# Interleaved split queries and keys, three loads for a head's operands, and a list scheduler with new instruction lengths

## The chip, the cores and the metric

The kernel runs on one core of one Trainium2 chip. The metric is device time in microseconds (us) of one execution. Before the change the median of three runs is 2257.74 us (2257.31 to 2260.61).

## The reference, cut to what matters

One encoder layer over 1024 tokens of width 1024, in float32: a half-step SwiGLU FFN, then attention beside an RWKV-7 scan on one joint input projection, then a second half-step FFN, each with RMSNorm before and after.

```python
x = x + 0.5 * post1(FFN1(pre1(x)))
z = pre2(x) @ w_in                       # 3456 columns: q|k|v and the RWKV inputs
x = x + post2(concat(attn, rwkv) @ w_out)
x = x + 0.5 * post3(FFN2(pre3(x)))
```

The attention has 8 heads of 64, rotary positions, and three dilated bands centred on the query. For the two narrow bands a query tile of 128 needs the scores

```python
s = jnp.einsum('bhrnqd,bhrnkd->bhrnqk', qb, kb)   # q . k over 64 dimensions
```

The RWKV-7 group runs a delta-rule scan over the sequence in both directions, for 8 heads.

## The kernel before, in words

**Precision by splitting.** TensorE multiplies in fp32r, a shortened float32. An f32 operand is split into a high part h (a copy cast to fp32r, on ScalarE) and a low part l (the rest, on VectorE), and a product is summed from h h, h l and l h. For the narrow-band scores the depth is only 64, so two parts are stacked to use all 128 rows of the array: `sq` holds q's high part on rows 0 to 63 and its low part on rows 64 to 127; `kh` holds k's high part twice and `kl` its low part twice. sq by kh plus sq by kl is (qh + ql)(kh + kl). `near` does these two matmuls for each piece of the scores (lines 1150 and 1151).

**Where these operands come from.** `project_tokens` (line 930) computes K, Q and V for the 8 token tiles and two groups of 256 columns each (16 units for each of the three, in the order K, Q, V). For a unit of K or Q it multiplies on TensorE, applies rotary positions on VectorE, turns the result on TensorE (`zt`) and makes three tiles of it: `zts` (f32), `zth` (high) and `ztl` (low), each of two buffers. Each goes to its own DRAM tensor with one GpSimd-issued store (lines 959 and 960): `q_d` and `kt_d` are lists of three, [4, 128, S], for f32, high and low. V's units take one store each (`d_va`).

`stacked` (line 1121) loads a head's operands when its turn comes: six loads on SyncE's queue, each of 64 rows of 4 KB. The wide band (`far`) works from the f32 copies, `qp` and `kp`, which are loaded for two heads at once with 128 rows.

**The stages.** FFN1; the RWKV projections (`zr` in the profile); the token projection (`zq`); attention and the scan side by side; the output projection; FFN2. In the scan, `prep` builds matrices of a block of tokens (`lp`, `lm`, `bp`), writes a part of them to DRAM (`d_x`), and `solve` (line 1316) loads them as `X` and inverts them in 31 pairs of short dependent steps (`ttmp`, `Ti`), on GpSimd for blocks 1 to 5 and on VectorE for blocks 0, 6 and 7. The result goes through DRAM (`d_t`, `d_tt`) into `merge` (`d`, `tt`, matmuls `pa`, `pb`), and `chain` carries the state (`xu`, `y`, `st`).

**Who sets the order.** The program is first written on a tape (`_Tape`, line 100); `order` (line 460) then plans the order of all instructions of the five queues (tensor, vector, scalar, gpsimd, sync) with a list scheduler, and `play` (line 486) issues them in that order. That is why every row of the profile has line 491. The planner works with a length of each instruction (`cost`, line 257): `took` is how long it holds its engine, `late` what passes after that until another engine can use the result, `moved` how long a transfer holds the DMA engines. `lag` (line 317) gives the delay from one instruction to one that depends on it; before the change that is zero on the same engine, transfers excepted. Among the ready instructions of a queue the one with the highest rank is taken (the longest way to the end, refined over five sweeps). The sweep has its own model of TensorE's clock, in 3413 ns steps. `LEADS` (line 37) is a table of (first, last, amount) by which the ranks of ranges of instructions are shifted before the last sweep.

Of the kernel before, what the change touches and what calls it, by code (L numbers as in the profile page):

```python
# [32 lines left out]
def _ap(src, off, pat):  # L33
# [3 lines left out]
LEADS = (  # L37
# [10 lines left out]
)  # L48
# [51 lines left out]
class _Tape:  # L100
# [156 lines left out]
    def cost(self, op):  # L257
# [8 lines left out]
        if op.method == "dma_start":  # L266
            runs = [math.prod(q[1] for q in a.ap) // (a.ap[-1][1] if a.ap[-1][0] == 1 else 1) for a in (x, *op.ins)]
            size = math.prod(q[1] for q in x.ap) * 4
            half = any(a.tensor.name in self.home and a.ap[0][1] <= 64 for a in (x, *op.ins))
            op.took, op.late = (560 if op.eng == "gpsimd" else 360) + 200 * half, 1500 + (600 if half else 0)  # L270
            op.moved = (14 * max(runs) + 0.0384 * size) / 16
        elif op.eng == "tensor":
# [13 lines left out]
            op.grid, op.cell = (up(k), up(m)), (at(w), at(x) if m <= 64 else 0)  # L286
            op.late = 170
        elif op.eng == "vector":
            rate = 1.04
            if op.method in ("tensor_copy", "tensor_scalar", "memset") and all(  # L290
                    self.home.get(a.tensor.name, (None,))[0].space != PSUM for a in op.ins if a.tensor.name in self.home):
                rate = 0.52
            if op.method in ("tensor_tensor_reduce", "tensor_reduce"):
                n = max(n, max(math.prod(q[1] for q in a.ap[1:]) for a in op.ins))
            if op.method == "tensor_tensor_scan":
                rate = 2.1
            op.took, op.late = 150 + rate * n + (83 if "accum_out" in op.kwargs else 0), 35
            op.port = sum(self.home.get(a.tensor.name, (None,))[0].space is None for a in op.ins
                          if a.tensor.name in self.home and math.prod(q[1] for q in a.ap[1:]) > 1) > 1
            if op.method == "reciprocal":  # L300
                op.took = 150 + 5 * n
        elif op.eng == "scalar":
            func = op.args[2] if op.method == "activation" else None
            aps = sum(isinstance(op.kwargs.get(k), bass.AP) for k in ("scale", "bias"))
            op.took = 170 + 0.87 * n + 95 * aps + (188 if "accum_out" in op.kwargs else 0)
            op.load, op.late = LOADS.get(func, 0), 40
        else:
            op.took, op.late, op.port = (200 + 2.1 * n if op.method != "memset" else 130 + 0.8 * n), 40, op.method != "memset"

    def pace(self, last, op, idle):  # L310

        took = op.took
        if op.grid != (128, 128) and (last is None or last.grid != op.grid or last.cell != op.cell):
            took /= 2
        return took + 95 if last and last.grid != op.grid and idle < 100 else took

    def lag(self, p, s):

        if p.eng is None or p.eng == s.eng and p.method != "dma_start":
            return 0.0  # L320
        return p.late + p.moved + (200 if s.eng == "gpsimd" else 0)

# [22 lines left out]
    def sweep(self, back=False):  # L345
# [29 lines left out]
        follow, last, port = None, None, 0.0  # L375
        while True:
# [26 lines left out]
            while op is None and heap[e]:  # L403
# [5 lines left out]
                if tag:  # L409
# [5 lines left out]
                    if at > t + 1e-6:  # L415
                        push(later[e], (at, -op.rank, op.n, op))
                        op = None
                        continue
                    slots[tag].remove(at)
            if op is None:  # L420
# [14 lines left out]
            if op.port:  # L435
                t = max(t, port)
                port = t + took
            op.start = t
            own = free[e] = t + took
            end = own  # L440
            if op.moved and not back:
                wire = max(wire, own) + op.moved
                end = wire - op.moved
            op.end = end
            out.append(op)
# [190 lines left out]
class _Kernel:  # L636
# [293 lines left out]
    def project_tokens(self, p, psum, x):  # L930

        nc, V, A, G, T = self.nc, self.nc.vector, self.nc.scalar, self.nc.gpsimd, self.nc.tensor
        for b, g in [(b, g) for b in (1, 0, 2) for g in range(2)]:
            hl = self.columns(p, b * 512 + g * 256, 256)
            for t in range(NT):
# [16 lines left out]
                for i in range(2):  # L952
                    T.transpose(q[:, i, :], of[:, i * 128:(i + 1) * 128], self.ident)
                y, h, l = (p.tile([128, 2, 128], dt, name="z" + n, tag="z" + n, bufs=2)
                           for n, dt in (("ts", F32), ("th", F32R), ("tl", F32R)))
                A.activation(h, q, AF.Copy)
                V.tensor_tensor(l, q, h, op=OP.subtract)
                A.activation(y, q, AF.Copy)
                for d, src in zip((self.q_d, self.kt_d)[b], (y, h, l)):
                    G.dma_start(d[g * 2:g * 2 + 2, :, ts].rearrange("a p t -> p a t"), src[:].bitcast(F32))  # L960

# [159 lines left out]
    def stacked(self, p, h):  # L1121

        ds = slice(h % 2 * 64, h % 2 * 64 + 64)
        (_, qh, ql), (_, kh, kl) = self.q_d, self.kt_d
# [8 lines left out]
    def near(self, psum, p, h, sq, kh, kl, v, far, between):  # L1133

# [7 lines left out]
        def scores(t):  # L1142
# [61 lines left out]
    def attention(self, psum, p):  # L1204
        X, F, ST = {}, {}, {}

        def load(pr):
# [6 lines left out]
            q, k = (p.tile([128, S], F32, name=n, tag=n) for n in ("qp", "kp"))  # L1214
            self.load(q, self.q_d[0][pr])
            self.load(k, self.kt_d[0][pr])
            X[pr] = q, k, v3, vn
# [348 lines left out]
    def constants(self):  # L1566
# [6 lines left out]
        for c, t in self.eps.items():  # L1573
# [11 lines left out]
        self.rk_d, self.v_d = self.dram("rk", [12, 128, S]), self.dram("v", [4, 128, S])  # L1585
        self.q_d, self.kt_d = ([self.dram(f"{nm}{c}", [4, 128, S]) for c in "fhl"]
                               for nm in ("q", "kt"))
        self.vt_d = self.dram("vt", [2, S, 2, 4, 64])
# [300 lines left out]
```

## Time and profile before

| | |
|---|---|
| median of three runs | 2257.74 us |
| profiled execution, whole | 2272.18 us |
| its span, first to last instruction | 2270.4 us |
| mean granted TensorE clock | 0.970 |
| attention's narrow-band score matmuls, first to last start | 1092 to 1392 us |
| bytes moved by DMA | 408.71 MB |

Rows of the profile name an engine (PE is TensorE, PEld its weight loads, DVE VectorE, ACT ScalarE, POOL GpSimd, SP SyncE), an operation, and out<-in by tile names with numbers left out, so that `sq`, `kh` and `kl` are the stacked operands and `s` both kinds of scores. POOLq and SPq are instructions that only issue a transfer. Rows of busy time by stretch give start and end, length, then the busy time and the count of instructions of each of the five engines (PE, PEld, DVE, ACT, POOL), the granted TensorE clock as a share of full speed, the share of the 16 DMA engines and GB/s. Rows in order of time give the start, the duration, and, in brackets, the idle time before it and what ended that. Rows on transfers end with the median of us from issue to landing.

### The profile page before, as it was taken

The numbers are of one execution on the slowest core, as the hardware profiler recorded it, in microseconds if no ns is written. First come the engines' busy times: TensorE is split into PE (matmuls) and PEld (weight loads), VectorE is DVE, ScalarE is ACT, GpSimd is POOL, SyncE is SP. The second block draws the span as 40 slices with busy tenths as digits, with TensorE's granted clock in tenths as the row PEclk, the third lists the DMA queues.
The fourth block names the chain that finished last, engine by engine and source line by source line (L and its number), as shares of the span: only waits on it lengthen the run. The fifth ranks groups of instructions, "written<-read, shape, count | busy, mean of one in ns | idle before, by whom it ended". The sixth has DMA issues, their size and how long they took to land.

```text
span 2270.4 us, 41200 instructions
## 1 busy us (share of the span) xinstructions
PE 2175.3 (96%) x15236; PEld 1799.2 (79%) x15236; DVE 1519.2 (67%) x2630; ACT 1051.3 (46%) x2023; POOL 720.1 (32%) x1038
## 2 busy tenths in 40 slices
PE   7999999999999999998989998898899999999998
PEld 5888888888887888898768777666688888888886
DVE  8877777775685477562635557647978777787566
ACT  6333333354576464543546566454533333335453
POOL 2244444520000010667373571221024444443000
PEclk9999999999999999999969799998999999999999
DMA  5355444586662377764967765587435544458665
GB/s 153 115 170 165 163 152 163 185 289 194 202 201 83 115 252 197 213 206 143 231 159 183 164 160 149 136 274 252 151 108 177 168 156 160 147 181 299 198 203 182
DMA packets 373053, 408.71 MB, mean 180 GB/s; under 512 B 76658, under 2 KB 279282, under 8 KB 372852
## 3 DMA queue, kind: packets, MB, share of 16 engines
q1 hardware_dynamic: 324096, 303.18, 45.2%
q0 software_dynamic: 30704, 94.44, 11.9%
q10 hardware_dynamic: 18052, 8.46, 1.4%
q8 instruction: 120, 1.97, 0.4%
q14 instruction: 81, 0.66, 0.1%
HBM read 271.69 MB, written 134.28 MB: 179 GB/s over the span
## 4 chain that ended last, share of the span: by engine, by line
PE 81%; DMA 6%; DVE 5%; POOL 2%; issue 2%; ACT 2%; SPq 1%; DVEq 0%; ACTq 0%; POOLq 0%
PE gu L491 37%; PE pd L491 17%; PE zr L491 5%; PE zq L491 5%; PE po L491 3%; PE pt L491 2%; PE lp L491 2%; DVE row L491 2%; PE s L491 2%; PE xu L491 2%; POOL Ti L491 1%; PE y L491 1%; POOL ttmp L491 1%; SPq L491 1%; DMA X<-d_x 1%
## 5 line engine op out<-in xcount | busy, mean ns | idle before, releaser
L491 ACT ACTIVATE wh<-raw 128x512 fp32r<-128x512 f32 x264 | 162.8, 628 | 373.5 <-PE gu L491 276.4
L491 POOL TENSOR_TENSOR row<-row 128x512 f32<-128x512 f32 x88 | 129.3, 1469 | 447.6 <-DVE row L491 420.2
L491 DVE TENSOR_TENSOR row<-gu,row 128x512 f32<-128x512 f32 x308 | 203.5, 685 | 101.1 <-PE gu L491 63.1
L491 DVE TENSOR_TENSOR wl<-raw,wh 128x512 fp32r<-128x512 f32 x264 | 214.5, 823 | 82.3 <-ACT wh L491 57.9
L491 PE MATMUL gu<-xh,wh 128*128 128x512 f32 x704 | 249.9, 394 | 3.6 <-ACT xh L491 1.5
L491 PE MATMUL gu<-xh,wl 128*128 128x512 f32 x704 | 250.6, 391 | 0.6 <-DVE wl L491 0.6
L491 PE MATMUL gu<-xl,wh 128*128 128x512 f32 x704 | 249.5, 393 | 0.0
L491 DVE TENSOR_TENSOR gwl<-graw,gwh 128x512 fp32r<-128x512 f32 (+1 forms) x176 | 116.4, 664 | 107.5 <-PE pd L491 76.0
L491 PE MATMUL pd<-gh,gwl 128*128 128x512 f32 x616 | 180.9, 391 | 0.5 <-DVE gwl L491 0.5
L491 PE MATMUL pd<-gl,gwh 128*128 128x512 f32 x616 | 180.0, 390 | 0.2 <-DVE gl L491 0.2
L491 PE MATMUL pd<-gh,gwh 128*128 128x512 f32 x616 | 180.2, 390 | 0.0
L491 ACT ACTIVATE gwh<-graw 128x512 fp32r<-128x512 f32 (+1 forms) x176 | 101.0, 577 | 137.0 <-PE pd L491 113.2
L491 PEld LDWEIGHTS gu<-xh,wh 128*128 128x128 f32 x704 | 132.9, 189 | 32.8 <-ACT xh L491 2.1
L491 PEld LDWEIGHTS gu<-xh,wl 128*128 128x128 f32 x704 | 132.3, 188 | 28.6 <-DVE wl L491 1.2
L491 PEld LDWEIGHTS gu<-xl,wh 128*128 128x128 f32 x704 | 132.6, 189 | 27.4 <-DVE xl L491 0.5
L491 PEld LDWEIGHTS pd<-gh,gwl 128*128 128x128 f32 x616 | 115.6, 188 | 25.3 <-DVE gwl L491 0.9
L491 PEld LDWEIGHTS pd<-gl,gwh 128*128 128x128 f32 x616 | 115.5, 188 | 24.7 <-DVE gl L491 0.6
L491 PEld LDWEIGHTS pd<-gh,gwh 128*128 128x128 f32 x616 | 115.5, 188 | 24.0
L491 ACT ACTIVATE gh<-raw 128x512 fp32r<-128x512 f32 x160 | 99.4, 629 | 57.0 <-PE pd L491 34.2
L491 DVE TENSOR_TENSOR gl<-raw,gh 128x512 fp32r<-128x512 f32 x160 | 115.7, 729 | 11.4 <-ACT gh L491 10.9
L491 POOL TENSOR_TENSOR ws<-ws 128x512 f32<-128x512 f32 x88 | 118.8, 1351 | 2.8
L491 POOL DMA_DIRECT2D d_hid<-row x154 | 83.8, 547 | 81.6 <-DVE row L491 67.6
(300 smaller groups left out, 5149.9 us busy)
## 6 DMA issues: line engine op xcount, KB each, us to landing
d_hid<-row POOLq DMA_DIRECT2D x154, 256.0 KB, 2.7
graw<-d_hid SPq DMA_DIRECT2D x132, 256.0 KB, 3.1
raw<-in_ffn_w_gate_dram SPq DMA_DIRECT2D x88, 256.0 KB, 3.0
raw<-in_ffn_w_up_dram SPq DMA_DIRECT2D x88, 256.0 KB, 3.1
ws<-in_ffn_w_down_dram SPq DMA_DIRECT2D x88, 256.0 KB, 3.7
d_ws<-ws POOLq DMA_DIRECT2D x88, 256.0 KB, 2.8
raw<-d_ws SPq DMA_DIRECT2D x88, 256.0 KB, 3.2
raw<-in_ffn_w_down_dram SPq DMA_DIRECT2D x66, 256.0 KB, 4.1
```

Of the source, the lines that this page charges most:

```text
L491: i = getattr(getattr(self.nc, op.eng), op.method)(*op.args, **op.kwargs).ins
```

## The change

1. *Layout.* The high and low parts of a unit lie in one tile `zt` of [128, 2, 2, 128], and go to DRAM tensors [8 heads, 64, 2, S] in which the two parts of each dimension are neighbours. K has one such tensor (`kk`: high, low). Q has two: `q1` (high, low) and `q2` (low, high), the same values with the parts exchanged. The stores of a K unit stay three (f32, and the pair in two halves), those of a Q unit become five.
2. *Loads.* `stacked` loads q1, q2 and kk of a head, each 128 rows of 4 KB in one transfer: three instead of six, the same bytes.
3. *Scores.* q1 by kk plus q2 by kk: (qh kh + ql kl) + (ql kh + qh kl).
4. *Planner.* New lengths for every kind of instruction; a delay between dependent instructions on one engine (TensorE excepted); at most eight transfers in flight for GpSimd's queue and eight for the others; 60 ns more for instructions that share a port; 100 ns more on TensorE when it changes to full-size fp32r tiles. `LEADS` is another table (29 ranges, where there were 45). So the order of every queue is planned anew.

```diff
-            op.took, op.late = (560 if op.eng == "gpsimd" else 360) + 200 * half, 1500 + (600 if half else 0)
-            op.moved = (14 * max(runs) + 0.0384 * size) / 16
+            op.took, op.late = 360 + 200 * (rows <= 64), 1700
+            if op.eng == "gpsimd":
+                op.took = 560 + 0.25 * max(runs)
+            runs = 6 * size / 4096 if op.eng == "gpsimd" else max(size / 4096, *runs)
+            op.moved = max((9.5 * runs + 0.0366 * size) / 16, size / (3.6 * rows))
...
-            op.took, op.late = 150 + rate * n + (83 if "accum_out" in op.kwargs else 0), 35
+            op.took, op.late = 68 + rate * n + 65 * (len(op.ins) > 2), 117
...
-            op.took = 170 + 0.87 * n + 95 * aps + (188 if "accum_out" in op.kwargs else 0)
-            op.load, op.late = LOADS.get(func, 0), 40
+            op.took, op.late = (68 if near else 111) + 0.833 * n + 90 * aps, 137
...
-            op.took, op.late, op.port = (200 + 2.1 * n if op.method != "memset" else 130 + 0.8 * n), 40, op.method != "memset"
+            op.took = 135 + 2.17 * n - min(n, 150) * 0.2 if op.method != "memset" else 110 + 0.8 * n
+            op.late, op.port = 134, op.method != "memset"
...
-        if p.eng is None or p.eng == s.eng and p.method != "dma_start":
+        if p.eng is None or p.eng == s.eng == "tensor":
             return 0.0
-        return p.late + p.moved + (200 if s.eng == "gpsimd" else 0)
+        if p.eng != s.eng:
+            return p.late + p.moved + (200 if s.eng == "gpsimd" else 0)
+        if p.moved and s.moved and all(a.tensor.name != p.out[0].tensor.name for a in s.ins):
+            return 0.0
+        return p.late + p.moved
...
+                if op.moved and not back and lanes[e == "gpsimd"][0] > t + 1e-6:
+                    push(later[e], (lanes[e == "gpsimd"][0], -op.rank, op.n, op))
+                    op = None
+                    continue
...
-                y, h, l = (p.tile([128, 2, 128], dt, name="z" + n, tag="z" + n, bufs=2)
-                           for n, dt in (("ts", F32), ("th", F32R), ("tl", F32R)))
+                y = p.tile([128, 2, 128], F32, name="zts", tag="zts", bufs=2)
+                w = p.tile([128, 2, 2, 128], F32R, name="zt", tag="zt", bufs=2)
+                h, l = w[:, :, 0], w[:, :, 1]
...
-                for d, src in zip((self.q_d, self.kt_d)[b], (y, h, l)):
-                    G.dma_start(d[g * 2:g * 2 + 2, :, ts].rearrange("a p t -> p a t"), src[:].bitcast(F32))
+                G.dma_start((self.q_d, self.kt_d)[b][g * 2:g * 2 + 2, :, ts].rearrange("a p t -> p a t"), y)
+                for d, v in zip(self.qk_d[b], (w, w[:, :, ::-1])):
+                    for i in range(2):
+                        G.dma_start(_ap(d, (g * 512 + i * 256) * S + t * 128, [[2 * S, 128], [S, 2], [1, 128]]),
+                                    v[:, i].bitcast(F32))
...
-        for nm, parts in (("sq", (qh, ql)), ("kh", (kh, kh)), ("kl", (kl, kl))):
+        for nm, src in zip(("q1", "q2", "kk"), (*self.qk_d[0], *self.qk_d[1])):
             t = p.tile([128, S], F32R, name=nm, tag=nm)
-            for j, src in enumerate(parts):
-                self.load(t[j * 64:j * 64 + 64].bitcast(F32), src[h // 2, ds, :])
+            self.load(t[:].bitcast(F32), _ap(src, h * 128 * S, [[S, 128], [1, S]]))
...
-                T.matmul(ps[:, :e - c], sq[:, qs], kh[:, k0 * 128 + c:k0 * 128 + e], start=True, stop=False)
-                T.matmul(ps[:, :e - c], sq[:, qs], kl[:, k0 * 128 + c:k0 * 128 + e], start=False, stop=True)
+                T.matmul(ps[:, :e - c], q1[:, qs], k[:, k0 * 128 + c:k0 * 128 + e], start=True, stop=False)
+                T.matmul(ps[:, :e - c], q2[:, qs], k[:, k0 * 128 + c:k0 * 128 + e], start=False, stop=True)
```

More of the change, by code (lines that the diff above doesn't have):

```diff
@@ L268, in cost @@
             size = math.prod(q[1] for q in x.ap) * 4
-            half = any(a.tensor.name in self.home and a.ap[0][1] <= 64 for a in (x, *op.ins))
-            op.took, op.late = (560 if op.eng == "gpsimd" else 360) + 200 * half, 1500 + (600 if half else 0)
-            op.moved = (14 * max(runs) + 0.0384 * size) / 16
+            rows = min(a.ap[0][1] for a in (x, *op.ins) if a.tensor.name in self.home)
+            op.took, op.late = 360 + 200 * (rows <= 64), 1700
[3 more added lines that the diff above has]
+            op.moved = max((9.5 * runs + 0.0366 * size) / 16, size / (3.6 * rows))
         elif op.eng == "tensor":
@@ L286, in cost @@
             op.grid, op.cell = (up(k), up(m)), (at(w), at(x) if m <= 64 else 0)
-            op.late = 170
+            op.late = 200
         elif op.eng == "vector":
@@ L296, in cost @@
                 rate = 2.1
-            op.took, op.late = 150 + rate * n + (83 if "accum_out" in op.kwargs else 0), 35
+            op.took, op.late = 68 + rate * n + 65 * (len(op.ins) > 2), 117
+            if "accum_out" in op.kwargs:
+                op.took, op.late = op.took + 8, 227
             op.port = sum(self.home.get(a.tensor.name, (None,))[0].space is None for a in op.ins
@@ L300, in cost @@
             if op.method == "reciprocal":
-                op.took = 150 + 5 * n
+                op.took = 68 + 5 * n
+            op.took += 110 * (x.ap[0][1] <= 64)
         elif op.eng == "scalar":
@@ L304, in cost @@
             aps = sum(isinstance(op.kwargs.get(k), bass.AP) for k in ("scale", "bias"))
-            op.took = 170 + 0.87 * n + 95 * aps + (188 if "accum_out" in op.kwargs else 0)
-            op.load, op.late = LOADS.get(func, 0), 40
-        else:
-            op.took, op.late, op.port = (200 + 2.1 * n if op.method != "memset" else 130 + 0.8 * n), 40, op.method != "memset"
+            near = all(self.home.get(a.tensor.name, (None,))[0].space == PSUM for a in op.ins[:1] if a.tensor.name in self.home)
+            op.took, op.late = (68 if near else 111) + 0.833 * n + 90 * aps, 137
+            if "accum_out" in op.kwargs:
+                op.took, op.late = op.took + 100, 230
+            op.took += 110 * (x.ap[0][1] <= 64)
+            op.load = LOADS.get(func, 0)
+        else:
+            op.took = 135 + 2.17 * n - min(n, 150) * 0.2 if op.method != "memset" else 110 + 0.8 * n
+            op.late, op.port = 134, op.method != "memset"
     def pace(self, last, op, idle):
@@ L314, in pace @@
             took /= 2
-        return took + 95 if last and last.grid != op.grid and idle < 100 else took
+        if last and last.grid != op.grid:
+            took += 95 * (idle < 100) + 100 * (op.grid == (128, 128) and op.args[1].dtype == F32R)
+        return took
     def lag(self, p, s):
-        if p.eng is None or p.eng == s.eng and p.method != "dma_start":
+        if p.eng is None or p.eng == s.eng == "tensor":
             return 0.0
-        return p.late + p.moved + (200 if s.eng == "gpsimd" else 0)
+        if p.eng != s.eng:
[3 more added lines that the diff above has]
+        return p.late + p.moved
     def rate(self):
@@ L374, in sweep @@
                     push(later[op.eng], (0.0, -op.rank, op.n, op))
-        follow, last, port = None, None, 0.0
+        follow, last, port, lanes = None, None, 0.0, ([0.0] * 8, [0.0] * 8)
         while True:
@@ L418, in sweep @@
                         continue
+                if op.moved and not back and lanes[e == "gpsimd"][0] > t + 1e-6:
+                    push(later[e], (lanes[e == "gpsimd"][0], -op.rank, op.n, op))
+                    op = None
+                    continue
+                if tag:
                     slots[tag].remove(at)
@@ L436, in sweep @@
                 t = max(t, port)
-                port = t + took
+                port = t + took + 60
             op.start = t
@@ L443, in sweep @@
                 end = wire - op.moved
+                lanes[e == "gpsimd"].append(wire + op.late)
+                lanes[e == "gpsimd"].pop(0)
             op.end = end
@@ L1121, in stacked, with near @@
     def stacked(self, p, h):
-        ds = slice(h % 2 * 64, h % 2 * 64 + 64)
-        (_, qh, ql), (_, kh, kl) = self.q_d, self.kt_d
         out = []
-        for nm, parts in (("sq", (qh, ql)), ("kh", (kh, kh)), ("kl", (kl, kl))):
+        for nm, src in zip(("q1", "q2", "kk"), (*self.qk_d[0], *self.qk_d[1])):
             t = p.tile([128, S], F32R, name=nm, tag=nm)
-            for j, src in enumerate(parts):
-                self.load(t[j * 64:j * 64 + 64].bitcast(F32), src[h // 2, ds, :])
+            self.load(t[:].bitcast(F32), _ap(src, h * 128 * S, [[S, 128], [1, S]]))
             out.append(t)
         return out
-    def near(self, psum, p, h, sq, kh, kl, v, far, between):
+    def near(self, psum, p, h, q1, q2, k, v, far, between):
         nc, V, A, G, T = self.nc, self.nc.vector, self.nc.scalar, self.nc.gpsimd, self.nc.tensor
@@ L1214, in load @@
             q, k = (p.tile([128, S], F32, name=n, tag=n) for n in ("qp", "kp"))
-            self.load(q, self.q_d[0][pr])
-            self.load(k, self.kt_d[0][pr])
+            self.load(q, self.q_d[pr])
+            self.load(k, self.kt_d[pr])
             X[pr] = q, k, v3, vn
@@ L1585, in constants @@
         self.rk_d, self.v_d = self.dram("rk", [12, 128, S]), self.dram("v", [4, 128, S])
-        self.q_d, self.kt_d = ([self.dram(f"{nm}{c}", [4, 128, S]) for c in "fhl"]
-                               for nm in ("q", "kt"))
+        self.q_d, self.kt_d = (self.dram(nm, [4, 128, S]) for nm in ("qf", "kf"))
+        self.qk_d = [[self.dram(nm, [H, 64, 2, S]) for nm in nms] for nms in (("q1", "q2"), ("kk",))]
         self.vt_d = self.dram("vt", [2, S, 2, 4, 64])
```

16 rows, old and new, of the table LEADS are left out of this document.

## The prediction, made before the changed kernel was run

> **What bounds the kernel now.** I read the page first, then busy time in stretches cut where the trace changes character, then the chain of waits inside the worst stretch.
>
> ```profile
> PE 2175.3 (96%) x15236; PEld 1799.2 (79%) x15236; DVE 1519.2 (67%) x2630; ACT 1051.3 (46%) x2023; POOL 720.1 (32%) x1038
> ...
> PEclk9999999999999999999969799998999999999999
> ```
> ```profile
> core 0: us, PE busy (x) PEld busy (x) DVE busy (x) ACT busy (x) POOL busy (x), PEclk, DMA share, GB/s
> ...
> 20.00:690.00 670.00, 664.05 (x2978) 546.34 (x2977) 488.70 (x736) 289.95 (x500) 193.87 (x222) 1.00 0.54 176
> 690.00:906.00 216.00, 212.99 (x1224) 178.57 (x1222) 129.98 (x231) 118.75 (x225) 12.68 (x26) 1.00 0.51 163
> 906.00:1068.00 162.00, 154.40 (x1608) 148.08 (x1606) 84.04 (x202) 69.15 (x184) 112.50 (x192) 0.98 0.62 184
> 1068.00:1400.00 332.00, 304.65 (x4796) 250.85 (x4796) 183.62 (x465) 197.67 (x450) 160.37 (x332) 0.88 0.72 173
> 1400.00:1640.00 240.00, 207.68 (x1864) 157.30 (x1863) 167.75 (x322) 119.12 (x228) 40.79 (x42) 0.91 0.66 208
> 1640.00:2250.00 610.00, 609.75 (x2701) 503.28 (x2700) 444.30 (x645) 236.42 (x403) 190.13 (x209) 1.00 0.55 179
> ```
>
> TensorE bounds the whole, but unevenly. In the two FFN stretches (20 to 690 and 1640 to 2250) it idles 6.0 and 0.3 us at full clock: no order of the same work finishes them sooner. The loss lies between. From 690 to 1640 the idle time is 3.0 + 7.6 + 27.4 + 32.3 = 70 us. There TensorE also runs below full clock: busy time by the missing part of the clock is 154.40 x 0.02 + 304.65 x 0.12 + 207.68 x 0.09 = 58 us. So some 128 us in all is what a better order could at most win, nine tenths of it after 1068, in attention with the scan (to 1400) and in what closes the mix (to 1640). Three narrower stretches:
>
> ```profile
> 1000.00:1060.00 60.00, 60.00 (x502) 59.96 (x501) 18.82 (x43) 15.96 (x47) 51.47 (x103) 1.00 0.44 132
> 1060.00:1080.00 20.00, 12.52 (x188) 11.70 (x188) 7.48 (x14) 10.66 (x22) 8.61 (x16) 0.74 0.80 207
> ...
> 1280.00:1300.00 20.00, 20.00 (x160) 16.28 (x160) 8.48 (x23) 7.12 (x16) 3.91 (x9) 0.61 0.52 117
> ```
>
> Up to 1060 the token projection covers everything; as it runs out TensorE has a hole of 7.5 us (20 less 12.52). What it waits for at that seam, and what the chain holds late in the same stage:
>
> ```profile
> 1067.30 1.63 POOL d_va L491 x3
> 1068.93 2.97 DMA d<-d_t
> ...
> 1298.97 0.52 SPq L491
> ...
> 1302.10 8.12 DMA X<-d_x
> ```
>
> GpSimd's queue is on the path at the seam (a load of the first solve's result stands behind three stores); SyncE's queue is on it for five issues in a row from 1298.97 until X's load starts to move, and the four ahead of X's are loads of a head's operands (the first and the last of the four, and X's):
>
> ```profile
> 1298.95 0.54 SPq L491 DMA_DIRECT2D sq<-d_qh  x1
> ...
> 1300.82 0.60 SPq L491 DMA_DIRECT2D kl<-d_ktl  x1
> 1301.58 1.11 SPq L491 DMA_DIRECT2D X<-d_x  x2
> ```
>
> **The change part by part.** Times are summed against the profiled execution: 2272.2 us, of which 2270.4 are span and 1.8 lie around it. It is 14.4 us above the median 2257.74 of the plain runs; I take a difference found in it over to the median unchanged.
>
> *Score products.* Two matmuls per piece before and after, each 128 rows deep with the same columns; q1 by k gives qh kh + ql kl, q2 by k the two mixed terms. The sum is the same four terms. Cost nothing: no row gains or loses an instruction.
>
> *Loads of a head, SyncE.* Six issues become three, eight heads: 24 fewer at 0.54 to 0.60 us, 14 us of queue. Most of it lies beside other work. On the chain stand the four issues of 1299: two of them go, 1.2 us. The other place is the start of attention, where head 1's six issues (the first and the last two of them below) precede the scan's next loads:
>
> ```profile
> 1083.33 0.67 SPq L491 DMA_DIRECT2D sq<-d_qh  x1
> ...
> 1086.70 1.24 SPq L491 DMA_DIRECT2D kl<-d_ktl  x2
> ```
>
> Half of six by 0.6 is 1.8 us. I take 3 us off, bounds 0 and 14.
>
> Landing time is the other half of this part:
>
> ```profile
> kh<-d_kth SPq DMA_DIRECT2D x16, 256.0 KB, 5.5
> kl<-d_ktl SPq DMA_DIRECT2D x16, 256.0 KB, 7.8
> ...
> kp<-d_ktf SPq DMA_DIRECT2D x4, 512.0 KB, 5.0
> ```
>
> A 128-row load of 512 KB lands in 5.0 us; a 64-row one of half the size takes 5.5, and kl, last of the six, 7.8. So a head's last operand may arrive 2.8 us sooner. I price it at nothing, because no row of TensorE's waits names these loads: ahead of the score matmuls it waits for VectorE's row minima most, and for no transfer:
>
> ```profile
> its engine sat idle before it (us, times) until:
>   DVE m L491: 16.2, 7
>   issue: 3.0, 4
> ...
> ```
>
> If the cover goes (a head wanted at once), 2.8 us by eight heads, 22 us, is the most to gain. [...]
>
> *Stores, GpSimd.* K keeps three stores per unit (f32 copy, and the interleaved pair as two halves). Q gets five instead of three, since q1 and q2 hold the same halves in the two orders: 16 units by 2 are 32 more.
>
> ```profile
> L491 POOL DMA_DIRECT2D d_qh<-zth x16: 707/718/751, 971.1 to 1065.2; - x16
> ```
> ```profile
> q0 software_dynamic: 30704, 94.44, 11.9%
> ```
>
> At 0.72 us they are 23 us more on GpSimd, all between 971 and 1067. The bytes are 32 by 128 KB, 4.2 MB; GpSimd's queue took 11.9% of 2270 us for 94.44 MB, 2.86 us a MB, so 12 us of the 16 engines in a stretch of 162 us with a share of 0.62: it becomes 0.69, hidden, cost nothing. GpSimd's time is not so free. The first of the 16 Q units and the first after 1000 are stored at
>
> ```profile
> 971.09 0.72 POOL L491 DMA_DIRECT2D d_qh<-zth  x1 [1.30 <-ACT zth L491]
> ...
> 1000.42 0.71 POOL L491 DMA_DIRECT2D d_qh<-zth  x1 [2.88 <-ACT zts L491]
> ```
>
> with seven units up to 1000, 4.2 us each, where five issues of 0.72, 3.6 us, find room. The nine units from 1000.42 on bring 18 more issues, 13 us, and in 1000 to 1060 GpSimd is free for 60 less 51.47, 8.5 us. The other work there is the first solve, whose result is what TensorE waits for at the seam. If nothing moves, 13 less 8.5, 4.5 us, comes out at the seam. Bounds: 0 (the planner stores more of Q before 1000, or V's units come between) and 13 (none of the free time is usable, since it falls between dependent steps). I take 4.5: the row of 1000 to 1060 is the place itself.
>
> *The planner's lengths.* All five queues are ordered anew over the whole kernel. Are the new lengths nearer to this chip? Starts of neighbours on VectorE and GpSimd:
>
> ```profile
> 299.71 0.68 DVE L491 TENSOR_TENSOR raw<-s,raw 128x512 f32<-128x512 f32 x1
> 300.31 0.68 DVE L491 TENSOR_TENSOR wl<-raw,wh 128x512 fp32r<-128x512 f32 x1
> ...
> 896.16 0.29 DVE L491 TENSOR_TENSOR ttmp<-X,Ti 128x126 f32<-128x126 f32 x1
> 896.49 0.29 DVE L491 TENSOR_TENSOR Ti<-Ti,ttmp 128x126 f32<-128x126 f32 x1
> ```
> ```profile
> 1021.05 0.47 POOL L491 TENSOR_TENSOR ttmp<-X,Ti 128x126 f32<-128x126 f32 x1
> 1021.60 0.50 POOL L491 TENSOR_TENSOR Ti<-Ti,ttmp 128x126 f32<-128x126 f32 x1
> ```
>
> Independent 512-wide steps start 0.60 us apart; the old length is 150 + 1.04 x 512 = 682 ns, the new 68 + 532 = 600. Dependent steps of 126 start 0.33 apart on VectorE and 0.55 on GpSimd; old 281 and 465 ns; new, with the delay that now also holds on one engine, 199 + 117 = 316 and 383 + 134 = 517. So the old plan takes VectorE for an eighth fuller than it is, and each solve (62 dependent steps) for 62 x 0.08, about 5 us, shorter than it is; five solves run on GpSimd. For transfers little improves: X's load is 0.56 + 2.79 by the old lengths and 0.56 + 2.84 by the new, against 8.1 us on the chain above. What is new there is the limit of eight transfers in flight to a queue.
>
> The chain of waits from 1060 to 1330, by line:
>
> ```profile
> by line: PE s L491 10.4%; PE lp L491 9.3%; POOL Ti L491 9.2%; POOL ttmp L491 8.7%; DMA X<-d_x 6.6%; PE pt L491 6.5%; PE po L491 5.8%; PE xu L491 5.3%; issue 5.3%; DMA in<-d_rk 3.4%; DMA d<-d_t 3.4%; PE y L491 3.2%; SPq L491 3.2%; PE st L491
> ```
>
> So the new plan knows better when a solve ends, which is what the order in 1068 to 1400 hangs on, but not when a load lands. What that is worth no row says. Its bounds: nothing won (or lost again, below) and the whole 128 us. I take a sixth, 21 us: the solves' steps are that share of the chain of waits in this stage (9.2% and 8.7%), and they are the links that are mis-sized.
>
> **Sum:** -3 + 4.5 - 21 = -19.5, so 2252.7 in the profiled execution and 2238 in the median.
>
> **The rivals.** *GpSimd becomes the bound at the seam (slower).* Place: 1000 to 1080. All 13 us of the nine late Q units fall on the first solve, because it is a chain of short dependent steps and every store that comes ready cuts into it. Both operand buffers of the pair are also held for four stores instead of two, so TensorE's copies cannot run ahead. The solve is 13 us late, TensorE has no cover left at the seam, and everything after it starts later. It decides as soon as the free time in 1000 to 1060 that the stores can really use is under 13 us and Q is not moved ahead. With 3 us from SyncE and nothing from the order: +10, 2268; without the 3 us, 2271. For it: 51.47 us of 60 taken. Against: the planner knows the price of a GpSimd issue, and V's units (one store each) can be put between.
>
> *The order only moves the holes.* Loads that land late stay mis-sized, X's and in's among them; the holes in 1068 to 1640 come back elsewhere. Then -3 + 4.5: 2259, no change.
>
> *The clock comes back with the holes (much faster).* If slow-clock stretches only follow idle time, each closed hole also returns its share of the 58 us. A third of the 70 us closed is 23, with 19 of clock: -42 + 1.5 gives 2217. For it: 1060 to 1080, idle 7.5 us and clock 0.74. Against it: 1280 to 1300, no idle time at all and clock 0.61, under short, narrow matmuls that the change keeps. [...]
>
> *Not what it says:* the diff leaves no room for six loads; I give this nothing.
>
> **How the numbers follow.** Forecast (-10 to -35 us) 0.58; clock 0.12; only moved 0.09; GpSimd 0.21. A measurement of this kernel can tell about 0.2%, 4.5 us, from no change. So faster 0.70, same 0.09, slower 0.21. The range leaves out the end of the clock rival below 2213 and what the GpSimd rival gives above 2269 when the order loses as well; 2213 to 2269 holds 8 in 10. Faster cases hold most of the chance; the forecast's own range is 2223 to 2248.
>
> **What would show it.** Right: 24 loads of 128 rows at about 0.6 us an issue; 128 Q and K stores at 0.72; POOL busy some 23 us more before 1070, a seam of at most 12 us; idle time and clock loss after 1068 together about 20 us less; both FFN stretches unchanged. Wrong: an FFN stretch in which TensorE now idles; the start of attention later by over 10 us; holes after 1068 as large as before, with the same loads as releasers.

## The result, and the profile after

| | before | after |
|---|---|---|
| median of plain runs | 2257.73 us | 2234.97 us (four runs, 2228.25 to 2237.71) |
| ratio, 95% interval | | 0.9892 [0.9869, 0.9915] |
| profiled execution, its span | 2272.18, 2270.4 us | 2235.32, 2233.5 us |
| mean granted TensorE clock | 0.970 | 0.982 |

The change takes 22.8 us off. The traces differ by more, 36.9 us of span: the profiled execution of before is 14 us above its plain median, in a second profile too (2272.71 us), and that of after is not. So about 14 us of what the two traces show apart are not in the medians (the plain runs of before beside the experiments lie mostly between 2250 and 2270); what makes them is not known.

The page of after, with the same two lines as were shown of before:

```profile
PE 2151.6 (96%) x15236; PEld 1780.8 (80%) x15236; DVE 1533.6 (69%) x2630; ACT 1044.2 (47%) x2023; POOL 730.6 (33%) x1070
...
PEclk9999999999999999999799999899999999999999
```

Busy time by stretch of after (columns as before):

```profile
20.00:690.00 670.00, 660.30 (x2939) 541.78 (x2939) 500.13 (x726) 280.22 (x487) 193.03 (x223) 1.00 0.54 174
690.00:906.00 216.00, 212.19 (x1183) 175.91 (x1182) 125.44 (x214) 119.36 (x226) 12.74 (x26) 0.98 0.52 165
906.00:1068.00 162.00, 155.59 (x1627) 151.15 (x1626) 87.21 (x223) 67.84 (x181) 125.84 (x214) 1.00 0.66 198
1068.00:1400.00 332.00, 311.55 (x5114) 258.55 (x5113) 205.35 (x522) 219.88 (x490) 165.23 (x343) 0.95 0.74 201
1400.00:1640.00 240.00, 221.27 (x1797) 168.71 (x1797) 173.69 (x327) 118.36 (x227) 41.74 (x43) 0.93 0.62 194
```

From 1068 to 1640 TensorE's idle time falls from 60 to 39 us (20.5 + 18.7), and what the clock costs from 55 to 31 us (311.55 x 0.05 + 221.27 x 0.07): 45 us less. Some of it was lost ahead: under the new order the first FFN and what closes it end later, and the RWKV projections start 8 us later.

```profile
L491 PE MATMUL zr<-xh,zh x192: 387/389/501, 712.7 to 879.6; 128*128 128x512 f32 x192
```
```profile
L511 PE MATMUL zr<-xh,zh x192: 387/389/794, 720.7 to 889.1; 128*128 128x512 f32 x192
```

(The first is before, the second after: shortest, middle and longest duration in ns, then first and last start.) -45 + 8 comes out at the 37 us of the spans.

To see where the time came from I cut each trace at two events: the last matmul of the token projection (`zq`), and the last of the scan's chain (`xu`, tile by tile as above; before, after, and the experiment *six_loads*, which is after with 64-row loads):

```profile
L491 PE MATMUL zq<-zh,xl x384: 278/283/416, 880.9 to 1063.5; 128*128 128x256 f32 x192
L491 PE MATMUL xu<-xs,tt x512: 213/218/366, 945.1 to 1509.4; 64*64 64x64 f32 x171
```
```profile
L511 PE MATMUL zq<-zh,xl x384: 278/283/385, 890.5 to 1068.3; 128*128 128x256 f32 x192
L511 PE MATMUL xu<-xs,tt x512: 216/218/363, 947.8 to 1487.4; 64*64 64x64 f32 x171
```
```profile
L512 PE MATMUL zq<-zh,xl x384: 278/283/385, 889.7 to 1067.7; 128*128 128x256 f32 x192
L512 PE MATMUL xu<-xs,tt x512: 216/218/363, 947.3 to 1504.1; 64*64 64x64 f32 x171
```

From the first to the second event, attention and the scan take 445.9 us before, 419.1 after and 436.4 in *six_loads*; from the second to the span's end it is 761.0, 746.1 and 746.5. The table behind the experiments has this cut for all of them. A cut at an event of one chain also counts work that an order moves from one side of it to the other, so the table gives what TensorE loses in each part as well.

### The profile page after: what moved, and what is told of

It reads as the page before. It is cut to its first block, busy times and chain, and to the rows that moved or that the text cites. A ratio compares the mean times of both kernels' runs of the same rounds, so it can differ in the third digit from the quotient of the medians.

```text
span 2233.5 us, 41237 instructions
## 1 busy us (share of the span) xinstructions
PE 2151.6 (96%) x15236; PEld 1780.8 (80%) x15236; DVE 1533.6 (69%) x2630; ACT 1044.2 (47%) x2023; POOL 730.6 (33%) x1070
## 4 chain that ended last, share of the span: by engine, by line
PE 80%; DMA 6%; DVE 6%; ACT 3%; issue 2%; POOL 1%; SPq 1%; DVEq 0%; ACTq 0%; POOLq 0%
PE gu L511 35%; PE pd L511 16%; PE zr L511 6%; PE zq L511 4%; PE po L511 3%; PE pt L511 3%; PE s L511 3%; DVE row L511 2%; PE lp L511 2%; PE op L511 2%; PE xu L511 1%; DMA wor<-in_w_out_dram 1%; PE st L511 1%; PE y L511 1%; DVE wl L511 1%
## 5 line engine op out<-in xcount | busy, mean ns | idle before, releaser
L511 DVE TENSOR_TENSOR wl<-raw,wh 128x512 fp32r<-128x512 f32 x264 | 236.3, 909 | 71.7 <-PE gu L511 38.0
L511 POOL TENSOR_TENSOR row<-row 128x512 f32<-128x512 f32 x88 | 122.3, 1390 | 416.5 <-DVE row L511 306.3
L511 PE MATMUL gu<-xh,wl 128*128 128x512 f32 x704 | 238.6, 392 | 0.2
L511 PE MATMUL gu<-xl,wh 128*128 128x512 f32 x704 | 235.1, 393 | 2.1 <-DVE xl L511 2.1
L511 PE MATMUL gu<-xh,wh 128*128 128x512 f32 x704 | 233.6, 393 | 3.1 <-ACT xh L511 3.1
```

The lines of the kernel that those rows point to most:

```text
L511: i = getattr(getattr(self.nc, op.eng), op.method)(*op.args, **op.kwargs).ins
```

## The experiments

**The theories.** *A, the order:* the new lengths and table earn the time, as forecast; the loads' form is worth a few issues on SyncE. *B, the loads:* a transfer to 64 rows is slower or holds something longer, and the three wide loads earn most of it. *C, the stores:* GpSimd pays for the 32 extra stores and the gain would be larger without them. (In the expectations of the first four kernels they are theories 1, 2 and 3.) In all kernels of this section but the two without a table and the two unchanged ones, the planner is that of after (in *old_order_new_layout* that of before) and works on the same program, and another transfer or matmul is issued in place of the planned one, so that the order stays:

```diff
-            i = getattr(getattr(self.nc, op.eng), op.method)(*op.args, **op.kwargs).ins
-            if op.eng in last:
...
+            for args in [op.args] if op.real is None else op.real:
+                i = getattr(getattr(self.nc, op.eng), op.method)(*args, **op.kwargs).ins
+                if op.eng in last:
...
```

Times are medians in us; ratios are to before on the same chip, run beside it, with their 95% interval. That interval is some 0.002 either way, so the difference of two ratios is known to about 0.003, 7 us.

**old_order_new_layout**: the old lengths, lag and table, so the old order; the new stores, loads and score matmuls issued in it (a store of a high or low part of Q becomes its two stores; of each pair of loads one is left out). Its stores hold one part of two heads' rows each, where after's hold both parts, in the same 512-byte pieces.

```diff
+            op.real = [(_ap(w, (g * 512 + ((c - 1) ^ swap)) * S + t * 128, [[2 * S, 128], [256 * S, 2], [1, 128]]),
+                                    src[:].bitcast(F32)) for swap, w in enumerate(self.qk_d[b])]
...
+            op.real = [] if j else [(t[:].bitcast(F32), _ap(new, h * 128 * S, [[S, 128], [1, S]]))]
```

> The planned order of before, instruction by instruction, with the new layout put into its places: K and Q stored interleaved (three and five stores), a head's operands loaded by three transfers of 128 rows at the place of the first of each old pair, the same score matmuls on q1, q2 and kk. Theory 1 (the new order of the queues brings nearly all of the gain, the layout nothing): 2259 us, between 2254 and 2265. Theory 2 (the three wide loads bring it, since they free SyncE's queue): 2240 us or less. Theory 3 (the 32 more stores cost GpSimd at the seam, the order must first earn that back): 2265 to 2272.

Measured: 2251.2, ratio 0.9975 [0.9959, 0.9992], between what A and B had said. The layout alone earns 5.6 us in the old order. Its trace is 31 us shorter between the two events (414.7 against 445.9), but some 18 us of that are in these two executions alone, which lie 14 us above and 4 us below their medians. It loses 8 us ahead of them: the last `zq` moves from 1063.5 to 1071.7.

**new_order_old_layout**: the new order; stores, 64-row loads and matmul operands as before.

```diff
+                        op.real = [] if j else [(self.hl_d[b][i][g * 2:g * 2 + 2, :, ts].rearrange("a p t -> p a t"),
+                                                 w[:, :, i].bitcast(F32))]
...
+            op.real = [(t[j * 64:j * 64 + 64].bitcast(F32), x[h // 2, h % 2 * 64:h % 2 * 64 + 64, :])
+                       for j, x in enumerate(dict(q1=(qh, ql), q2=(kh, kh), kk=(kl, kl))[nm])]
...
+                op.real = [(ps[:, :e - c], q1[:, qs], q2[:, k0 * 128 + c:k0 * 128 + e])]
...
```

> The planned order of after with the old layout put into its places: high and low parts in tensors of their own, three stores for a unit of Q too, six loads of 64 rows per head (two where after has one), the stacked products. Theory 1: 2233 us, between 2229 and 2240. Theory 2: 2250 us or more. Theory 3: below 2228, since the stores are gone.

Measured: 2243.78, ratio 0.9945 [0.9925, 0.9965]. The order alone earns 12 us, about half of the whole and between what A and B had said. Its trace has 434.7 us between the events and 741.4 us from there to the end; where the order pays is read from the table below.

**six_loads**: after, with each wide load as two of 64 rows, upper half and lower half.

```diff
+            op.real = [(t[j:j + 64].bitcast(F32), _ap(src, (h * 128 + j) * S, [[S, 64], [1, S]])) for j in (0, 64)]
```

> After, order unchanged, each of the three loads of a head issued as two of 64 rows in its place; stores and layout of after. Theory 1: 3 us at most above after, 2235 to 2238. Theory 2: 2245 or more. Theory 3 says nothing on it.

Measured: 2250.09, ratio 0.9967 [0.9950, 0.9984]: about 15 us of the gain are gone with the same order, stores and matmuls. So B holds against A's view of the loads. What in them costs that was open: the issues, or the rows.

**no_q2_stores**: after, with the 32 stores of q2 left out and q2 loaded from q1.

```diff
+                        op.real = [] if j else None
...
+                op.real = [(t[:].bitcast(F32), _ap(self.qk_d[0][0], h * 128 * S, [[S, 128], [1, S]]))]
```

> After, order unchanged, without the 32 stores of q2; q2 is loaded from q1 instead, the same bytes, so the score products leave out the mixed high-low terms. Theory 1: 0 to 4.5 us below after, 2230 to 2235. Theory 3: 2225 or less. Theory 2: the same as after.

Measured: 2234.15, ratio 0.9903 [0.9885, 0.9920], against after's 0.9892 and 0.9907. The kernel leaves out the mixed high-low products. Its last `zq` comes at 1065.1, 3.2 us ahead of after's 1068.3 and 6.7 ahead of the 1071.8 of *after_again*; nothing of it can be told at the end. C falls as a cost of the whole, and the term at the seam is some 3 to 7 us.

**after_again** and **before_again**: both unchanged, for the spread.

> After, unchanged, so that it stands beside the other variants on one chip. 2235 us, ratio to before 0.989; six narrow loads at the same order gave 2250.

> Before, unchanged, for a second trace of it. The first profiled execution was 14 us above the median of the plain runs; if that is chance, this one comes out nearer to 2258, and the narrow-band scores end before 1392 us.

Measured: after 2236.37, ratio 0.9907 [0.9883, 0.9931]; before, profiled, 2272.71 with a span of 2270.9. The gain repeats, and so does the excess of before's profiled execution.

**six_by_columns**: six transfers again, but each of 128 rows by half the columns.

```diff
+            op.real = [(t[:, j:j + 512].bitcast(F32), _ap(src, h * 128 * S + j, [[S, 128], [1, 512]])) for j in (0, 512)]
```

> After, order unchanged, each of the three loads of a head cut into two of 128 rows and half the columns: six issues in SyncE's queue as with the narrow loads, but every transfer reaches all rows. Theory Q (what the narrow loads cost is the number of transfers in SyncE's queue): 2250 us, as with six narrow loads. Theory S (it is the 64-row form, which moves at half the rate): as after, within 4 us.

Measured: 2238.54, ratio 0.9912 [0.9889, 0.9934]. With 24 more issues on SyncE and the same size a transfer as in *six_loads*, the gain stays: neither the number of issues nor the size is what costs. (The half rate of theory S is that of before's landings: 256 KB to 64 rows took 5.5 us in the median (`kh`), 512 KB to 128 rows 5.0 (`kp`).)

**halves_on_act**: *six_loads*, with the second half of each issued by ScalarE, so SyncE has 24 issues as in after.

```diff
+            op.real = [(eng, (t[j:j + 64].bitcast(F32), _ap(src, (h * 128 + j) * S, [[S, 64], [1, S]])))
+                       for eng, j in (("sync", 0), ("scalar", 64))]
```

> After, order unchanged, each load as two of 64 rows, but the second of the two is issued by ScalarE: SyncE has three issues per head again, the form is the narrow one. Theory Q: within 4 us of after. Theory S: 2245 to 2250 us.

Measured: 2255.63, ratio 0.9997 [0.9981, 1.0013], above the range expected. Fewer issues on SyncE bring nothing back; two queues for the two halves do not either. What makes it some 7 us slower than *six_loads* was not separated.

**six_even_odd**: six transfers of 64 rows, but the even and the odd rows, not the upper and the lower ones.

```diff
+            op.real = [(t[j::2].bitcast(F32), _ap(src, (h * 128 + j) * S, [[2 * S, 64], [1, S]])) for j in (0, 1)]
```

> After, order unchanged, each load of a head cut into two of 64 rows, but the even rows and the odd rows of the tile, not its upper and lower half. Six issues of 256 KB, 64 descriptors of 4 KB each, as with the six narrow loads that gave 2250. [...]

Measured: 2238.33, ratio 0.9902 [0.9879, 0.9925]. This is the sharpest of them: the same 64 rows, 4 KB rows, count and queue as *six_loads*, and the whole gain: 0.9902, where *six_loads* had 0.9967. So it is not the count of 64 rows. What costs here is that a transfer reaches only the upper or the lower half of the partitions. (The rows read from DRAM differ too: a half's lie in one piece, the even ones do not; but after's loads, in one piece like the halves, cost nothing.) The landings of the two kernels in all (copies, KB each, median us), *six_loads* first:

```profile
q<-d_q SPq DMA_DIRECT2D x32, 256.0 KB, 6.5
kk<-d_kk SPq DMA_DIRECT2D x16, 256.0 KB, 6.4
```
```profile
q<-d_q SPq DMA_DIRECT2D x32, 256.0 KB, 5.1
kk<-d_kk SPq DMA_DIRECT2D x16, 256.0 KB, 5.2
```

And the stretch of attention beside the scan, *six_loads*, *six_even_odd*, *halves_on_act* in this order:

```profile
1068.00:1400.00 332.00, 303.31 (x5015) 252.87 (x5016) 189.94 (x481) 213.01 (x479) 163.35 (x342) 0.92 0.77 194
```
```profile
1068.00:1400.00 332.00, 312.40 (x5110) 259.74 (x5108) 199.38 (x504) 218.86 (x490) 166.79 (x345) 0.94 0.73 198
```
```profile
1068.00:1400.00 332.00, 305.12 (x5035) 256.43 (x5035) 182.31 (x462) 208.91 (x472) 167.74 (x353) 0.91 0.77 189
```

Read the last two columns together: share by GB/s is the time that the 16 DMA engines are held for a MB. It is 0.77 / 194 = 3.97 us a MB in *six_loads* and 4.07 in *halves_on_act* (4.16 before, by its row of 0.72 and 173), but 3.69 in *six_even_odd* and 3.68 in after (0.74 and 201). With whole or evenly spread rows the engines move 2 to 6% more bytes in the stretch and are held less for them. By their edits *six_loads* (3.97) and *six_even_odd* (3.69) differ only in which 64 rows a transfer moves.

The traces also hold each single packet. From 1068 to 1400 a packet of 4 KB (a row of a head's load, or of `qp` or `kp`) takes 281 ns in the median before, 266 in *six_loads* and 265 in *new_order_old_layout*, but 159 in *old_order_new_layout*, *six_even_odd* and after; all other packets take 29 to 30 ns on average in each of them. Where a head's 384 packets run in one row, they take 8.0 to 8.4 us in the first three and 4.9 to 6.8 in the last two, with up to some 20 under way at a time in either. So no fewer engines seem to be at work, and a transfer to one half holds each of them longer, by the 266 ns against 159. What they wait for in that time is not shown.

How the cost gets to TensorE is shown in part. The matmuls of after and of *six_loads* come in nearly the same order and can be compared one by one: *six_loads* is 0.6 us ahead at 1066, then 7.7 us behind at 1131, 13.4 at 1251 and 17.3 at 1393, and stays there. So the loss arises where the heads are loaded. By the rows above it is 8 us of idle time (28.7 against 20.5) and 9 us of clock (303.31 x 0.08 against 311.55 x 0.05). Of TensorE's waits for a transfer there, one grows by over 1 us (*six_loads*, then after: us, times, longest):

```profile
PE s L512 <- DMA kp<-d_kf: 6.4, 1, 6.4
```
```profile
PE s L511 <- DMA kp<-d_kf: 3.9, 1, 3.9
```

The rest is spread over many waits, most of them for VectorE and ScalarE. Some other loads land later too (from 1060 to 1400, *six_loads* and after):

```profile
th_a<-d_a SPq DMA_DIRECT2D x10, 256.0 KB, 5.2
...
qp<-d_qf SPq DMA_DIRECT2D x4, 512.0 KB, 6.5
vn<-d_va SPq DMA_DIRECT2D x4, 512.0 KB, 9.6
```
```profile
th_a<-d_a SPq DMA_DIRECT2D x10, 256.0 KB, 3.6
...
qp<-d_qf SPq DMA_DIRECT2D x4, 512.0 KB, 4.4
vn<-d_va SPq DMA_DIRECT2D x4, 512.0 KB, 6.9
```

But `X` does not (4.1 in both), and in *halves_on_act* `th_a` lands in 3.9 and `vn` in 7.2, though that kernel is the slowest of the three. So which of these delays TensorE pays for is not shown.

**after_no_leads** and **before_no_leads**: the table emptied, so that the lengths alone set the order.

```diff
-        for a, b, lead in LEADS:
+        for a, b, lead in ():
```

> After with an empty table of shifts: the last sweep by the new lengths alone. If the new lengths bring what the order gains (theory L): within 6 us of after, 2242 at most. If the table does (theory T): 2250 or more.

> Before with an empty table of shifts, the old lengths alone. Theory L: above after without its table by 20 us or more, 2262 to 2275. Theory T: the two planners without tables differ by the layout alone, some 10 us.

Measured: 2240.51, ratio 0.9902 [0.9879, 0.9925], and 2283.7, ratio 1.0102 [1.0081, 1.0122]. The old table had earned 23 us on the old lengths; the new one earns nothing that these intervals show. Without tables the two kernels are 43 us apart, of which 6 to 12 are the layout's by the ratios of this section. So what the order brings lies in the new planner's lengths, delays and limits, not in its table, and 23 us of it the old table had already made up for.

**wide_x_v**: an attempt to go on. `X` and the `v3` pairs are also loaded as two times 64 rows; here each pair is one transfer of 128 rows whose DRAM pattern repeats or steps over an outermost dimension of 2.

```diff
+            op.real = [] if q else [(X.rearrange("p a b -> p (a b)"), _ap(self.x_d[n % 4], 0, [[0, 2], [1024, 64], [1, 1024]]))]
...
+                op.real = [] if j else [(v3, _ap(self.v_att, pr * 128, [[512, 2], [16 * 512, 64], [2 * 512, 8], [1, 128]]))]
```

> After, order unchanged, two other kinds of 64-row loads made wide as well: the pair that loads X (the same 256 KB twice, 8 solves) becomes one transfer of 128 rows, and so does the pair that loads v3 (4 times). If the 64-row form itself is what cost (theory S: 12.6 MB in narrow loads cost about 15 us), these 6.3 MB give 4 to 8 us: 2227 to 2232, and X lands sooner than 4.6 us after its last issue. If the form only matters where a head's operands collide with everything else, the same as after.

Measured: 2326.81, ratio 1.0297 [1.0271, 1.0322], so 67 us slower than before. On its chain of waits (start, us):

```profile
892.03 14.99 DMA X<-d_x
1016.89 17.48 DMA X<-d_x
1186.43 25.48 DMA X<-d_x
```

The six `X` on that chain take 13 to 25 us each, where the two halves of after land in 4.1 us each. GpSimd's solves then stand for it (idle us, times, longest), in this kernel from 1068 to 1480 and in after from 1068 to 1400:

```profile
POOL ttmp L512 <- DMA X<-d_x: 113.6, 4, 48.5
```
```profile
POOL ttmp L511 <- DMA X<-d_x: 56.2, 4, 33.6
```

A transfer to 128 rows is thus not enough by itself. In the last of these loads, from 1492 to 1504, the 128 packets of 4 KB run two at a time (159 ns each, so at least 10 us for 64 in a row); of after's `X` mostly 16 are under way at once. The new pattern has an outermost dimension of 2; that this makes the two was not shown, since no run here varied that dimension alone. The share of the `v3` loads was not separated. No version that computes the whole beat after.

**All but wide_x_v, cut at the two events** (one profiled execution each, us; "lost" is TensorE's idle time plus its busy time by the missing part of the clock):

| kernel | order | a head's loads reach | last `zq` | to last `xu` | of it lost | to the end | of it lost |
|---|---|---|---|---|---|---|---|
| before, before_again | old | half | 1063.5, 1063.6 | 445.9, 446.8 | 87, 92 | 761.0, 760.5 | 28, 28 |
| old_order_new_layout | old | all | 1071.7 | 414.7 | 52 | 759.4 | 28 |
| before_no_leads | old lengths | half | 1069.9 | 442.5 | 85 | 767.8 | 40 |
| new_order_old_layout | new | half | 1064.1 | 434.7 | 64 | 741.4 | 18 |
| six_loads, halves_on_act | new | half | 1067.7, 1073.7 | 436.4, 440.3 | 66, 70 | 746.5, 742.1 | 24, 19 |
| after, after_again | new | all | 1068.3, 1071.8 | 419.1, 419.8 | 48, 49 | 746.1, 743.4 | 23, 21 |
| six_by_columns, six_even_odd | new | all | 1070.9, 1070.9 | 422.9, 422.6 | 53, 52 | 744.9, 743.4 | 23, 21 |
| no_q2_stores | new | all | 1065.1 | 421.8 | 52 | 744.2 | 21 |
| after_no_leads | new lengths | all | 1072.7 | 423.7 | 59 | 748.9 | 24 |

The length up to the last `xu` splits by the loads' rows, whatever the order (415 to 424 against 435 to 447), the one from there to the end by the order, whatever the loads (741 to 749 against 759 to 768). But the new order also moves work: behind the last `xu` 3296 matmuls are left in after and 3376 in before, which is about 10 us of TensorE's time (721.9 us busy there against 731.7). So of the 15 us at the end about 10 are work done earlier, and 4 to 10 are less loss. Between the events the new order does that work as well and with half loads still loses less (64 to 70 us against 85 to 92, of which up to 14 in the two of before are not in the medians); with whole loads the old order loses 52 there and the new one 48 to 59, no difference that shows.

## Why the prediction was right, and where its steps were not

The time fell by 22.8 us where 19.5 were forecast. That it fits so well is luck: the sum came out by two errors that cancel, one in the loads' landing and one in the order.

**Loads, issues: right.** 24 issues, shorter even than the 0.6 us expected, as the diff's `took` had them (360 ns, and 200 more up to 64 rows; shortest, middle, longest in ns):

```profile
L511 SPq DMA_DIRECT2D q<-d_q x16: 319/423/1758, 1074.0 to 1289.5; - x16
```

Their number hardly counts: with all 48, *six_by_columns* is 2.2 us above *after_again* on the same chip, no more than the intervals allow.

**Loads, landing: the step that failed.** "I price it at nothing, because no row of TensorE's waits names these loads." The runs put about 15 us there: 0.9967 for *six_loads* against 0.9892 and 0.9907 is 14 to 17 us. A list of waits names the last releaser of one engine; what these loads took was time of the DMA engines, and it came out as a longer stay of the work beside the scan (436.4 us between the two events in *six_loads*, 419.1 in after). Upper and lower halves in turn did not make up for each other: a head's loads held the engines for 8.0 to 8.4 us, in place of 4.9 to 6.8. A hint of it stood in the prediction: a share of 0.72 for 173 GB/s, 4.16 us a MB against 3.1 to 3.4 in the other five long stretches; but after still has 3.68 there, so only half of that excess was these loads. The diff itself priced it: the new `moved` is at least the bytes by 3.6 times the rows, which makes a head's loads six times 1138 ns with 64 rows and three times 1275 ns with 128. The bound of 22 us, kept out of the sum, was the nearer end.

**Stores: right in size at the seam, nothing at the end.** +4.5 expected at the seam, 3 to 7 measured with *no_q2_stores*, and none of it seen at the end. The seam of after, with 4.2 + 4.3 us idle in two stretches, as against 7.5 + 0.8 before, so within the 12 us named:

```profile
1060.00:1080.00 20.00, 15.84 (x213) 14.83 (x213) 6.04 (x11) 8.22 (x19) 14.80 (x30) 0.88 0.59 169
1080.00:1100.00 20.00, 15.67 (x200) 13.89 (x197) 10.16 (x19) 10.49 (x21) 2.60 (x4) 0.59 1.09 319
```

The DMA share from 906 to 1068 rose to 0.66, not to 0.69. POOL's busy time there rose by 13 us (112.50 to 125.84), not by 23, because by the profile, which is rough on GpSimd, issues now overlap its steps (below).

**The slower rival was real, under the old order.** In *old_order_new_layout* the five stores of a unit stand in one block ahead of a step of the first solve, this solve lasts 56.3 us with 40 issues in it, against 48.7 with 28 before, the seam comes 8 us later, and TensorE loses its cover from 1000 to 1060 (55.52 us busy where it had 60.00). In order of time on GpSimd:

```profile
1015.31 0.33 POOL L492 TENSOR_TENSOR ttmp<-X,Ti 128x81 f32<-128x81 f32 x1
1015.78 1.47 POOL L492 DMA_DIRECT2D d_q<-zth  x2
1017.25 0.73 POOL L492 DMA_DIRECT2D d_qf<-zts  x1
1017.97 1.45 POOL L492 DMA_DIRECT2D d_q<-ztl  x2
1019.44 0.41 POOL L492 TENSOR_TENSOR Ti<-Ti,ttmp 128x81 f32<-128x81 f32 x1
```

After's own plan puts one store between two dependent steps, where its new delay on one engine leaves a gap:

```profile
1027.64 1.07 POOL L511 DMA_DIRECT2D d_q<-zt  x1
1028.26 0.86 POOL L511 TENSOR_TENSOR Ti<-Ti,ttmp 128x96 f32<-128x96 f32 x1
1028.59 1.17 POOL L511 DMA_DIRECT2D d_q<-zt  x1
1029.22 0.96 POOL L511 TENSOR_TENSOR ttmp<-X,Ti 128x115 f32<-128x115 f32 x1
```

So the first solve, which starts 10 us later, lasts 49.5 us with 37 issues in it; in *no_q2_stores*, in the same order with 27, it lasts 50.2. By the ratios the layout is worth 5.6 us in the old order and 9 to 12 in the new (0.9945 against 0.9907 and 0.9892); that goes with this, though the intervals overlap.

**Order: a little too high, and not only in the place named.** -21 was forecast; it is -12 with the old layout and -15 to -19 with the new one (0.9975 against 0.9907 and 0.9892). It was to come from 1068 to 1400, through better lengths of the solves. By the table some of it lies there (with half loads 64 to 70 us lost up to the last `xu`, against 85 to 92), and 4 to 10 us lie behind. Behind it TensorE stood for GpSimd's part of the scan's output less (before, then after, 1400 to 1640; idle us, times, longest):

```profile
PE yc L491 <- POOL f_y L491: 7.7, 5, 5.3
```
```profile
PE yc L511 <- POOL f_y L511: 5.7, 3, 2.8
```

That is 2 us; which of the new lengths, delays or limits does the rest was not separated and stays open.

**What was to show it.** "Both FFN stretches unchanged" was wrong for the first: its last matmul (`pd`) comes at 679.8 where it came at 673.9 (679.5 and 675.0 in the second profiles), and the projections behind it start 8 us later. Idle time and clock after 1068 fell by 45 us in the traces, not by 20; up to 14 of them are not in the medians. *The clock rival* had 23 us of holes and 19 of clock; the traces show 21 and 24, so the clock did come back with the holes, but with the 8 us lost ahead and the 14 that are not in the medians the time stayed near the forecast. The row held against this rival, 1280 to 1300, does not speak against it: that half clock (a granted 0.5 in the trace) begins at 1271.7, with 1.4 us idle in the 7 us ahead, and goes on to 1295.6, though TensorE is busy without a hole from 1276. All eleven stretches at half clock that begin between 1060 and 1440 in the two traces have 0.9 to 3.3 us idle in the 7 us ahead of them. *Only moves the holes* is out: new_order_old_layout's 0.9945 lies below its 1.

## What to carry to other kernels

Try a transfer into SBUF that reaches rows of both halves, even if it must be cut in two: here even and odd rows (0.9902) or columns (0.9912) kept the gain, the upper and the lower 64 rows (0.9967) lost 14 to 17 us of it. Look at DMA share by GB/s in each stretch, since such a loss may appear in no list of waits (here 3.97 us a MB against 3.69 showed it). When a trace is cut at an event, see whether the same work lies on either side of it before a gain is put down to a place. What an added DMA issue costs on an engine with a chain of short dependent steps may hang on its place: on GpSimd here 12 more issues, in blocks, made the first solve 7.6 us longer (*old_order_new_layout* against before), and 10 more, singly between steps, made it no longer (after's 49.5 us against the 50.2 of *no_q2_stores*).

## What the runs showed of the hardware that was not expected

- Two 64-row loads (upper, lower) in succession landed in 6.5 us each in the median (*six_loads*, `q`) and cost this kernel 14 to 17 us over 24 pairs; even and odd rows of the same size landed in 5.1 us (*six_even_odd*) and cost nothing that shows.
- A packet of 4 KB took 159 ns in transfers that reach both halves, and 265 to 281 in the median where the heads' loads reach one.
- In before, a clock of 0.5 outlasted the hole ahead of it: 20 us of TensorE busy without idle (1276 to 1295.6), under short, narrow matmuls, before the clock was 1.0 again.
- A GpSimd issue took 0.72 us by itself (before's `d_qh` stores), 0.9 to 1.5 between dependent steps by the profile's rough spans (after's `d_q`), and then ran beside them: step and issue together started every 0.9 to 1.3 us, where 0.55 + 0.72 had been added up. All issues of the interleaved tensors (shortest, middle, longest in ns):

```profile
L511 POOL DMA_DIRECT2D d_q<-zt x64: 668/888/1457, 965.2 to 1069.7; - x64
```

- A SyncE issue to 128 rows took 0.42 us (after's `q`, median), one to 64 rows 0.54 to 0.60 (before's `sq` and `kl`).
- In *wide_x_v* the 512 KB loads of `X`, whose DRAM pattern has an outermost dimension of 2, stood for 13 to 25 us on the chain of waits, in the last of them with two packets at a time.
